# A two-layer hybrid decoder in float32: transition from attention to MLP, and the tail, in another order

## Chip, cores and metric

One core of a Trainium2 chip. The metric is the device time of one execution in microseconds, the median of three runs. A profile was taken of one further execution; all times in the rows come from that one, counted from the start of its span.

## What is computed

Two layers on 256 tokens of width 1024, all in float32. Each layer is an attention part with three kinds of heads, whose outputs form a mixture of 1024 columns (`mix`), and a gated MLP with a causal convolution over tokens. Cut to what matters here:

```python
for i in range(DEPTH):                               # DEPTH = 2
    h = rmsnorm(x, norm1_g[i])
    mix = hybrid_mixer(h, w_in[i], ...)
    x = x + mix @ w_out[i]                           # output projection, 1024 x 1024
    h = rmsnorm(x, norm2_g[i])
    x = x + conv_glu_ffn(h, w_up[i], ..., w_down[i]) # up 1024 -> 2 x 2816, down 2816 -> 1024
return rmsnorm(x, final_g)
```

## The kernel before

The tokens stand as two tiles of 128 rows (t = 0, 1); the residual `xr` stays on the chip. A float32 product is made of three products of rounded parts: each operand is split into a high and a low part, and hi x hi, hi x lo and lo x hi are added up in a PSUM bank (`mm3`, L201, L202, L203). Weights come in pieces through `weight` (L143 to L149): SyncE issues a load into one of 5 staging tiles `st`, ScalarE rounds it to the high part (L147), VectorE subtracts to get the low part (L149), both into one of 8 tiles `hl`. Activations are turned by `transposed`: TensorE transposes 128 x 128 blocks into a bank (L182), ScalarE scales and rounds them (L188), VectorE makes the low part (L189), both into `ahl`.

The source is written stage by stage. A scheduler sets the final order on each engine; engines run their queues in order and wait on each other by semaphores. `dense` holds generators of products that `fill` draws on between other steps, and the scheduler interleaves them with the attention's work.

The places that matter:

- **Output projection**, `out_part`. It is called twice, for the first three weight groups and for the last two (`GROUPS[3:]`). For each half n of the output columns (512) two banks `bd` are open, one per token tile; the groups of weights are walked one by one, with both tiles inside each, and then both banks are added to `xr` (L800).
- **Attention's last product**, 24 matmuls (L848); its output is split by ScalarE (L359) and VectorE (L360), and the second call of `out_part` needs it.
- **`half2(n)`**: squares of the half n of `xr` on ScalarE (L172, by `sumsq`), transposes, evacuations. From the squares GpSimd makes `rstd2` (L165 to L167), and a product with the identity spreads it over columns (L873, `R`).
- **`up(f)`**, one of 11 iterations per layer over the MLP's 2816 hidden columns, 256 at a time: four banks `bu` (two halves s by gate and value, au), each the sum of 8 products of 512 columns (L904) and 8 of 256 (L906). The 8 blocks are the 1024 features, and `ks` says which of them a step takes. In iteration 0 the two banks of s = 0 are walked in two halves of the features, the two of s = 1 whole. Then come convolution, gate and `h_hi`, `h_lo`. `down(f - 1)` follows `up(f)` and adds into four banks `bn`.
- **The tail**, behind the last layer: the last two iterations' down products bank by bank, add (L953), square on ScalarE, multiplication with the final gain (L991), power on GpSimd (L995), scale by ScalarE (L996) and VectorE (L998), and output by two queues (L997, L999), 512 columns each.

```python
order = [(au, s, range(8)) for au in range(2) for s in range(2)]
if f == 0:
    order = [(0, 0, range(4)), (1, 0, range(4)), (0, 0, range(4, 8)), (1, 0, range(4, 8)),
             (0, 1, range(8)), (1, 1, range(8))]
```

Of the kernel before, what the change touches and what calls it, by code (L numbers as in the profile page):

```python
# [76 lines left out]
def trunk(ctx, tc, x, w_in, cmp_w1, cmp_w2, w_out, w_up, w_down, final_g, gains, params, eye, consts_f, consts_b, out):  # L77
# [127 lines left out]
    for i in range(DEPTH):  # L205

        with ExitStack() as es:
# [578 lines left out]
            def out_part(*groups):  # L786
                ks = sum(groups, ())
                for n in range(2):
                    bs = [bank("d"), bank("d")]
                    for g in groups:  # L790
                        wh, wl = weight(piece(w_out[i], (8 * n + g[0]) * 128 * 512, 128, len(g) * 512), len(g), 512)
                        for k in g:
                            for t in range(2):
                                q = slice(t * 128, (t + 1) * 128)
                                mm3(bs[t], mhi[k // 4][:, k % 4, q], mlo[k // 4][:, k % 4, q], wh[:, k - g[0]],
                                    wl[:, k - g[0]], k == ks[0], k == ks[-1])
                        yield
                    for t in range(2):
                        xs = xr[:, t, n * 512:(n + 1) * 512]
                        V.tensor_tensor(xs, bs[t], xs, op=OP.add)  # L800
                yield
# [78 lines left out]
        with ExitStack() as es:  # L880
# [7 lines left out]
            def up(f):  # L888
                wh = [weight(w_up[i, f, au, h], 4, 256)
                      for au in range(2) for h in range(2)]  # L890
                wd = [weight(w_down[i, (2 * f + s) * 128:(2 * f + s + 1) * 128, :], 1, 1024) for s in range(2)]
                order = [(au, s, range(8)) for au in range(2) for s in range(2)]
                if f == 0:
                    order = [(0, 0, range(4)), (1, 0, range(4)), (0, 0, range(4, 8)), (1, 0, range(4, 8)),
                             (0, 1, range(8)), (1, 1, range(8))]
                bs, sums = {}, [mp.tile([128, 2, L], F32, name=n, tag=n) for n in ("sa", "su")]
                for au, s, ks in order:
# [4 lines left out]
                    w = [[z[:, k % 4, s * 128:(s + 1) * 128] for z in wh[2 * au + k // 4]] for k in ks]  # L902
# [38 lines left out]
            def down(fs, which):  # L941
                for n, t in which:
                    for f in fs:
                        h_hi, h_lo, wd = hs[f]
                        for s in range(2):
                            wh, wl = wd[s]
                            q, c = slice(t * 128, (t + 1) * 128), slice(n * 512, (n + 1) * 512)
                            mm3(dn[n, t], h_hi[:, s, q], h_lo[:, s, q], wh[:, 0, c], wl[:, 0, c],
# [88 lines left out]
```

## Time and profile before

| what | value |
|---|---|
| median of 3 runs | 651.7 us (651.59 to 652.59) |
| profiled execution | 651.93 us |
| its span | 650.1 us |
[...]
| TensorE busy | 631.1 us, 97% |
| VectorE busy | 531.6 us, 82% |
| ScalarE busy | 399.3 us, 61% |
| GpSimd busy | 48.0 us, 7% |
| chain that ended last | TensorE 78%, VectorE 14%, ScalarE 3% |

The span runs from the first to the last recorded instruction; 1.8 us of the execution lie around it. Layer 0's transition from attention to MLP lies at about 118 to 154 us, layer 1's at about 435 to 471 us, the tail from 634 us on. A busy share is the time in which at least one instruction's record is open. [...]

### The profile page before, as it was taken

Reading aid. Unit: us, or ns where it says so; the run is one execution under the profiler, and the core shown is the slowest. Engines: PE = TensorE matmul, PEld = TensorE weight load, DVE = VectorE, ACT = ScalarE, POOL = GpSimd, SP = SyncE. Lnnn points to the kernel's source line nnn. Section 1 sums busy time; section 2 is a strip of 40 time slices with the busy share of each in tenths; the row PEclk is TensorE's granted clock in tenths of the full one; section 3 lists DMA queues with packets and bytes.
Section 4 is the critical chain, followed back from the end, with each engine's and each line's share of the span. In section 5 each row is a group of like instructions: output and inputs, shape, how many; then the busy total and the mean of one; then the engine's idle time right before and its main releaser. Section 6 shows DMA issues by size and latency. Waiting matters only on the chain.

```text
span 650.1 us, 10491 instructions
## 1 busy us (share of the span) xinstructions
PE 631.1 (97%) x3694; PEld 538.3 (83%) x3694; DVE 531.6 (82%) x1180; ACT 399.3 (61%) x773; POOL 48.0 (7%) x115
## 2 busy tenths in 40 slices
PE   7989999999999999999999999999999999999995
PEld 6978887778888888888898888867788888888884
DVE  5989999786877778888787799987598787777773
ACT  6666578666555555555575666785665555555533
POOL 0322210000000000000020241000000000000002
PEclk9999999999999999999999999999999999999998
DMA  8971424454666666655466425235367666566601
GB/s 282 331 237 50 148 65 115 161 172 143 203 196 195 192 191 185 189 189 166 121 182 219 144 70 167 83 106 169 115 180 233 190 183 191 191 194 195 193 2 65
DMA packets 32500, 107.28 MB, mean 165 GB/s; under 512 B 3776, under 2 KB 4032, under 8 KB 31936
## 3 DMA queue, kind: packets, MB, share of 16 engines
q1 hardware_dynamic: 31536, 104.77, 51.5%
q0 software_dynamic: 336, 1.05, 0.4%
q10 hardware_dynamic: 576, 0.79, 0.4%
q8 instruction: 29, 0.48, 0.3%
q14 instruction: 23, 0.19, 0.1%
HBM read 105.55 MB, written 1.05 MB: 164 GB/s over the span
## 4 chain that ended last, share of the span: by engine, by line
PE 78%; DVE 14%; ACT 3%; issue 2%; POOL 1%; DMA 1%; POOLq 0%; SPq 0%; DVEq 0%; ACTq 0%
PE bu L904 24%; PE bu L906 13%; PE bn L201 6%; PE bn L202 6%; PE bn L203 6%; PE bd L201 5%; PE bd L203 4%; PE bd L202 4%; DVE hl L149 4%; PE bt L365 1%; PE bs L345 1%; DVE acc L477 1%; DVE P L753 1%; ACT hl L147 1%; DVE m L476 1%
## 5 line engine op out<-in xcount | busy, mean ns | idle before, releaser
L149 DVE TENSOR_TENSOR hl<-st,hl 128x1024 fp32r<-128x1024 f32 (+3 forms) x208 | 232.1, 1120 | 58.6 <-ACT hl L147 58.1
L147 ACT CAST hl<-st 128x1024 fp32r<-128x1024 f32 (+3 forms) x208 | 201.4, 972 | 120.1 <-PE bn L203 43.5
L904 PE MATMUL bu<-ahl,hl 128*128 128x512 f32 x704 | 177.9, 393 | 2.0 <-DVE ahl L189 2.0
L904 PEld LDWEIGHTS bu<-ahl,hl 128*128 128x128 f32 x704 | 127.2, 189 | 25.9 <-DVE ahl L189 2.8
L906 PEld LDWEIGHTS bu<-ahl,hl 128*128 128x128 f32 x704 | 96.7, 190 | 7.1
L906 PE MATMUL bu<-ahl,hl 128*128 128x256 f32 x704 | 99.3, 282 | 0.0
L201 PE MATMUL bd<-hl,ahl 128*128 128x384 f32 (+2 forms) x256 | 92.6, 366 | 1.9 <-ACT hl L147 1.0
L202 PE MATMUL bd<-hl,ahl 128*128 128x384 f32 (+2 forms) x256 | 91.6, 358 | 0.4 <-DVE hl L149 0.4
L203 PE MATMUL bd<-hl,ahl 128*128 128x384 f32 (+2 forms) x256 | 91.5, 357 | 0.0
L201 PE MATMUL bn<-hl,h_hi 128*128 128x512 f32 x176 | 69.0, 392 | 0.1
L202 PE MATMUL bn<-hl,h_hi 128*128 128x512 f32 x176 | 68.7, 391 | 0.0
L203 PE MATMUL bn<-hl,h_lo 128*128 128x512 f32 x176 | 68.5, 389 | 0.0
L909 ACT COPY cross<-bu 128x256 f32<-128x256 f32 x88 | 32.5, 370 | 39.9 <-PE bu L906 39.6
L201 PEld LDWEIGHTS bd<-hl,ahl 128*128 128x128 f32 x256 | 48.1, 189 | 9.9 <-ACT hl L147 2.6
L202 PEld LDWEIGHTS bd<-hl,ahl 128*128 128x128 f32 x256 | 48.3, 189 | 3.8 <-issue 1.1
L203 PEld LDWEIGHTS bd<-hl,ahl 128*128 128x128 f32 x256 | 48.2, 188 | 3.4 <-issue 1.2
L921 DVE SCALAR_TENSOR_TENSOR c<-a,cols,c 128x255 f32<-128x255 f32 (+1 forms) x88 | 40.0, 481 | 7.5 <-ACT c L919 6.3
L203 PEld LDWEIGHTS bn<-hl,h_lo 128*128 128x128 f32 x176 | 33.0, 188 | 7.3 <-DVE h_lo L934 0.3
L201 PEld LDWEIGHTS bn<-hl,h_hi 128*128 128x128 f32 x176 | 33.1, 188 | 7.1 <-ACT h_hi L933 0.9
L202 PEld LDWEIGHTS bn<-hl,h_hi 128*128 128x128 f32 x176 | 33.1, 188 | 6.0
L919 ACT ACTIVATE c<-a,cols 128x256 f32<-128x256 f32 x44 | 24.1, 595 | 13.5 <-DVE a L913 13.5
L910 DVE TENSOR_TENSOR sa<-bu,cross 128x256 f32<-128x256 f32 x44 | 18.4, 417 | 6.5 <-ACT cross L909 4.4
(235 smaller groups left out, 781.8 us busy)
## 6 DMA issues: line engine op xcount, KB each, us to landing
st<-in_w_up_dram SPq DMA_DIRECT2D x88, 512.0 KB, 4.0
st<-in_w_down_dram SPq DMA_DIRECT2D x44, 512.0 KB, 4.3
st<-in_w_in_dram SPq DMA_DIRECT2D x40, 384.0 KB, 4.0
st<-in_w_out_dram SPq DMA_DIRECT2D x12, 512.0 KB, 3.8
w<-in_cmp_w_dram SPq DMA_DIRECT2D x4, 1024.0 KB, 8.4
st<-in_w_in_dram SPq DMA_DIRECT2D x8, 360.0 KB, 3.4
st<-in_w_in_dram SPq DMA_DIRECT2D x8, 336.0 KB, 3.4
st<-in_w_out_dram SPq DMA_DIRECT2D x8, 256.0 KB, 3.1
```

Source lines behind the costliest of these rows:

```text
L147: S.copy(hv, sv)
L149: V.tensor_sub(lv, sv, hv.bitcast(F32))
L201: PE.matmul(b, ahi, whi, start=first, stop=False)
L202: PE.matmul(b, ahi, wlo, start=False, stop=False)
L203: return PE.matmul(b, alo, whi, start=False, stop=last)
L345: PE.matmul(b[:, o:o + nk], qa, ka, start=True, stop=True)
L904: PE.matmul(o, wa, hhl[k // 4][:, k % 4].rearrange("p z t -> p (z t)"), start=k == 0, stop=False)
L906: PE.matmul(o[:, :L], wl, hhi[k // 4][:, k % 4, :], start=False, stop=k == 7)
L909: S.copy(cross, o[:, L:])
L910: V.tensor_tensor(sums[au][:, s], o[:, :L], cross, op=OP.add)
L919: S.activation(c[:, o:o + 256], a[:, o:o + 256], AF.Identity, bias=cw[3], scale=cw[2])
L921: V.scalar_tensor_tensor(c[:, o + d:o + 256], a[:, o:o + 256 - d], cw[w], c[:, o + d:o + 256], op0=OP.mult, op1=OP.add)
```

## The change

- `out_part`: the last two groups of a half n are walked token tile by token tile. Both groups' products of t = 0 are made, its bank is added, and then the same for t = 1. (For the second call, which has two groups, that is all of it.) One `fill` step less is drawn before `half2`.
- `half2`: the transposes are written ahead of the squares, and the last evacuations are returned as `ready`.
- `up(0)`: the weights come as (gate, first half of the features), (value, first half), (gate, second half), (value, second half), and the latter two are cast only behind `ready`. All four banks take the first half of the features, then all four the second.
- Tail: the bank (1, 1) is closed two iterations early and added (L965 there); its last two iterations go into fresh banks `bu`, in two halves of 256 columns. The last square is made on VectorE. The scaled output is split as 384 columns (ScalarE, SyncE's queue) and 640 (VectorE, ScalarE's queue).

```diff
             def out_part(*groups):
...
                     for g in groups:
+                        ws[g] = weight(piece(w_out[i], (8 * n + g[0]) * 128 * 512, 128, len(g) * 512), len(g), 512)
+                        if g in groups[:-2]:
                             for t in range(2):
+                                products(t, g)
+                            yield
                     for t in range(2):
+                        for g in groups[-2:]:
+                            products(t, g)
                         xs = xr[:, t, n * 512:(n + 1) * 512]
                         V.tensor_tensor(xs, bs[t], xs, op=OP.add)
+                        yield
...
-            fill(3)
+            fill(2)
...
             def half2(n):
+                for k0 in (0, 2):
+                    last = transposed(bank, xr, gain2[i], hhi, hlo, 4 * n + k0, 2)
                 for t in range(2):
                     sumsq(ssq, t, n)
-                for k0 in (0, 2):
-                    transposed(bank, xr, gain2[i], hhi, hlo, 4 * n + k0, 2)
+                return [z.ins for z in last]
...
-            half2(0)
+            ready = half2(0)
...
             def up(f):
-                wh = [weight(w_up[i, f, au, h], 4, 256)
-                      for au in range(2) for h in range(2)]
+                wh = {}
+                for au, h in ((0, 0), (1, 0), (0, 1), (1, 1)) if f == 0 else ((0, 0), (0, 1), (1, 0), (1, 1)):
+                    wh[au, h] = weight(w_up[i, f, au, h], 4, 256, behind=ready if (f, h) == (0, 1) else (None, None))
...
                 if f == 0:
-                    order = [(0, 0, range(4)), (1, 0, range(4)), (0, 0, range(4, 8)), (1, 0, range(4, 8)),
-                             (0, 1, range(8)), (1, 1, range(8))]
+                    order = [(au, s, ks) for ks in (range(4), range(4, 8)) for s in range(2) for au in range(2)]
...
+                    f1 = NF - 3 if i == DEPTH - 1 and (n, t) == (1, 1) and into is None else NF - 1
...
+            add(1, 1)
...
+                pieces = [(0, 0, 512), (1, 0, 512)] if t == 0 else [(0, 0, 512), (1, 0, 256), (1, 256, 512)]
+                for j, (n, a, b) in enumerate(pieces):
+                    last = j == len(pieces) - 1
+                    o = None if b - a == 512 else bank("u1")[:, :b - a]
+                    down(fs, [(n, t)], slice(a, b), o)
+                    xs = add(n, t, slice(a, b), o)
...
+                    if last and t:
+                        V.scalar_tensor_tensor(junk[:, :b - a], xs, 1.0, xs, op0=OP.mult, op1=OP.mult,
+                                               accum_out=sq[:, j:j + 1])
+                    else:
+                        S.activation(junk[:, :b - a], xs, AF.Square, accum_out=sq[:, j:j + 1])
...
+                S.activation(y[:, 0:384], y[:, 0:384], AF.Copy, scale=r)
+                nc.sync.dma_start(out[0, t * 128:(t + 1) * 128, 0:384], y[:, 0:384])
+                V.tensor_scalar(y[:, 384:D], y[:, 384:D], r, None, op0=OP.mult)
+                nc.scalar.dma_start(out[0, t * 128:(t + 1) * 128, 384:D], y[:, 384:D])
```

How the order moves. TensorE, layer 0, from the last product of the output projection to the second bank of `up(0)` (`bd` is the projection's bank, `bu` one of `up`, `bt` a transpose's; lines 904 and 906 are 914 and 916 after the change, 182 is the transposes). Before:

```order
L203 MATMUL bd<-hl,ahl 128x512
L904 MATMUL bu_1862<-ahl,hl 128x512
L904 MATMUL bu_1871<-ahl,hl 128x512
L904 MATMUL bu_1902<-ahl,hl 128x512
L904 MATMUL bu_1924<-ahl,hl 128x512
L182 MATMUL bt<-ident,xr 128x128
L904 MATMUL bu_1862<-ahl,hl 128x512 x2
L182 MATMUL bt<-ident,xr 128x128
L904 MATMUL bu_1862<-ahl,hl 128x512
L906 MATMUL bu_1862<-ahl,hl 128x256 x2
L182 MATMUL bt<-ident,xr 128x128 x6
L906 MATMUL bu_1862<-ahl,hl 128x256 x2
```

With the change:

```order
L203 MATMUL bd<-hl,ahl 128x512
L182 MATMUL bt<-ident,xr 128x128 x2
L914 MATMUL bu_1862<-ahl,hl 128x512 x4
L916 MATMUL bu_1862<-ahl,hl 128x256 x3
L182 MATMUL bt<-ident,xr 128x128 x6
L916 MATMUL bu_1862<-ahl,hl 128x256
L914 MATMUL bu_1871<-ahl,hl 128x512 x4
L916 MATMUL bu_1871<-ahl,hl 128x256 x4
L914 MATMUL bu_1880<-ahl,hl 128x512 x4
L916 MATMUL bu_1880<-ahl,hl 128x256 x4
```

Two transposes of the second half now stand ahead of the first up product, which starts with four products of one bank instead of one of each of the four; the banks follow one another, each with the first four blocks of the features alone.

ScalarE, layer 0, from the split of the attention's last output (L359) to the first banks of `up(0)`: casts of weights (L147), squares (L172), evacuations of transposes (L188), the spread row scale (L875, then L884) and evacuations of `up` (L909, then L919). Before:

```order
L359 CAST ahl<-bo 128x2x256
L147 CAST hl<-st 128x1024 x4
L172 ACTIVATE junk,ssq<-xr 128x512 x2
L147 CAST hl<-st 128x1024
L188 ACTIVATE ahl<-bt,cols 128x256 x2
L147 CAST hl<-st 128x1024
L188 ACTIVATE ahl<-bt,cols 128x256 x2
L172 ACTIVATE junk,ssq<-xr 128x512 x2
L188 ACTIVATE ahl<-bt,cols 128x256 x4
L875 COPY R<-bt 128x256
L909 COPY cross<-bu_1862 128x256
L909 COPY cross<-bu_1871 128x256
```

With the change:

```order
L359 CAST ahl<-bo 128x2x256
L172 ACTIVATE junk,ssq<-xr 128x512 x2
L188 ACTIVATE ahl<-bt,cols 128x256 x4
L147 CAST hl<-st 128x1024
L172 ACTIVATE junk,ssq<-xr 128x512
L147 CAST hl<-st 128x1024 x2
L172 ACTIVATE junk,ssq<-xr 128x512
L188 ACTIVATE ahl<-bt,cols 128x256 x2
L147 CAST hl<-st 128x1024 x2
L188 ACTIVATE ahl<-bt,cols 128x256 x2
L147 CAST hl<-st 128x1024 x2
L884 COPY R<-bt 128x256
```

The four casts ahead of the squares and the cast amid the first evacuations have gone behind them; four of the casts now stand among the squares and evacuations of the second half.

VectorE, the tail's second token tile: adds to the residual (L953, then L965), gain (L991, then L1022), sum of the means (L994, then L1018), square (L1012), scale (L998, then L1026). Before:

```order
L953 TENSOR_TENSOR xr<-bn_5262,xr 128x512
L953 TENSOR_TENSOR xr<-bn_5264,xr 128x512
L991 TENSOR_TENSOR y_6976<-xr,fg 128x512
L994 SCALAR_TENSOR_TENSOR fin_6973<-ssq,fin_6972 128x1
L998 TENSOR_SCALAR y_6976<-y_6976,fin_6974 128x512
```

With the change:

```order
L965 TENSOR_TENSOR xr<-bn_5262,xr 128x512
L965 TENSOR_TENSOR xr<-bu_6997,xr 128x256
L1022 TENSOR_TENSOR y<-xr,fg 128x256
L1018 SCALAR_TENSOR_TENSOR fin_6975<-fins_6977,fin_6974 128x1
L965 TENSOR_TENSOR xr<-bu_7015,xr 128x256
L1012 SCALAR_TENSOR_TENSOR junk,fins_6977<-xr 128x256
L1018 SCALAR_TENSOR_TENSOR fin_6976<-fins_6977,fin_6975 128x1
L1022 TENSOR_TENSOR y<-xr,fg 128x256
L1026 TENSOR_SCALAR y<-y,finr_6978 128x640
```

The second add has become two of 256 columns, from banks of `up`; the last one is followed by its square on VectorE, and its gain stands behind the sum instead of ahead of it.

## Rows read from the trace of the kernel before

**Rows 1.** Busy time by stretch: start:end, length, busy us (count) per engine, PEclk, DMA share, GB/s.
```profile
128.00:154.00 26.00, 24.35 (x129) 19.58 (x128) 17.17 (x26) 16.43 (x30) 2.42 (x11) 1.00 0.45 139
154.00:300.00 146.00, 146.00 (x779) 126.11 (x778) 121.06 (x176) 86.02 (x129) 0.00 (x0) 1.00 0.63 194
```

**Rows 2.** TensorE's timeline, layer 0: start us, us, line, operation, out<-in, count [idle before].
```profile
127.98 0.50 PE L203 MATMUL bd<-hl,ahl 128*128 128x512 f32 x1
...
130.16 0.47 PE L201 MATMUL bd<-hl,ahl 128*128 128x512 f32 x1 [0.29 <-DVE xr L800]
...
134.13 0.39 PE L203 MATMUL bd<-hl,ahl 128*128 128x512 f32 x1
134.63 0.50 PE L201 MATMUL bd<-hl,ahl 128*128 128x512 f32 x1
...
137.96 0.82 PE L182 MATMUL bt<-ident,xr 128*128 128x128 f32 x6
138.53 0.48 PE L202 MATMUL bd<-hl,ahl 128*128 128x512 f32 x1
...
139.53 0.39 PE L203 MATMUL bd<-hl,ahl 128*128 128x512 f32 x1
140.91 1.21 PE L904 MATMUL bu<-ahl,hl 128*128 128x512 f32 x4 [0.99 <-DVE ahl L189]
...
154.03 2.00 PE L904 MATMUL bu<-ahl,hl 128*128 128x512 f32 x8
```

**Rows 3.** Chain of waits, layer 0: start us, us, engine, tile, line.
```profile
128.10 0.60 ACT ahl L359
128.72 0.69 DVE ahl L360
...
138.16 1.06 ACT hl L147
139.24 0.77 DVE hl L149
...
140.38 0.87 DVE ahl L189 x2
...
150.67 0.95 PE bu L906 x8
```

**Rows 4.** TensorE's timeline, layer 1.
```profile
447.48 0.47 PE L201 MATMUL bd<-hl,ahl 128*128 128x512 f32 x1 [0.18 <-DVE xr L800]
...
471.33 2.00 PE L904 MATMUL bu<-ahl,hl 128*128 128x512 f32 x8
```

**Rows 5.** Timeline of the tail, last layer.
```profile
643.07 0.39 PE L203 MATMUL bn<-hl,h_lo 128*128 128x512 f32 x1
643.50 0.69 DVE L953 TENSOR_TENSOR xr<-bn,xr 128x512 f32<-128x512 f32 x1 [1.89 <-PE bn L203]
...
644.29 0.63 ACT L172 ACTIVATE junk<-xr 128x512 bf16<-128x512 f32 x1 [1.86 <-DVE xr L953]
644.82 0.19 ACT L172 ACTIVATION_READ_ACCUMULATOR junk<-xr 128x1 f32 x1
...
645.95 0.72 ACT L996 ACTIVATE y<-y,fin 128x512 f32<-128x512 f32 x1 [0.94 <-POOL fin L995]
...
646.69 0.34 SPq L997 DMA_DIRECT2D out_dram<-y  x1
```

**Rows 6.** ScalarE's timeline, layer 0: evacuations of two transposes.
```profile
139.11 0.83 ACT L188 ACTIVATE ahl<-bt,cols 128x256 fp32r<-128x256 f32 x2
```

**Rows 7.** Timeline of SyncE's DMA queue, layer 0.
```profile
131.77 1.59 SPq L143 DMA_DIRECT2D st<-in_w_up_dram  x2
```

**Rows 8.** DMA issues, 154 to 300 us: tile, queue, count, size, median us to landing.
```profile
st<-in_w_up_dram SPq DMA_DIRECT2D x34, 512.0 KB, 4.2
```

**Rows 9.** Costliest groups of the page: out<-in count | busy us, mean ns | idle before.
```profile
L910 DVE TENSOR_TENSOR sa<-bu,cross 128x256 f32<-128x256 f32 x44 | 18.4, 417 | 6.5 <-ACT cross L909 4.4
```

**Rows 10.** Line 251: duration ns min/median/max, first and last start.
```profile
L251 DVE SCALAR_TENSOR_TENSOR junkv<-xr x2: 678/684/691, 14.5 to 15.2; 128x512 bf16<-128x512 f32 x2
```

More of the change, by code (lines that the diff above doesn't have):

```diff
@@ L900, in up @@
                         o = bs[au, s] = bank(f"u{au}")
-                    w = [[z[:, k % 4, s * 128:(s + 1) * 128] for z in wh[2 * au + k // 4]] for k in ks]
+                    w = [[z[:, k % 4, s * 128:(s + 1) * 128] for z in wh[au, k // 4]] for k in ks]
                     for k, (wa, _) in zip(ks, w):
@@ L939, in trunk, with down @@
                     dn[n, t] = bank(f"n{n}")
-            def down(fs, which):
+            def down(fs, which, part=slice(0, 512), into=None):
                 for n, t in which:
+                    f1 = NF - 3 if i == DEPTH - 1 and (n, t) == (1, 1) and into is None else NF - 1
                     for f in fs:
@@ L994, in trunk @@
-                V.scalar_tensor_tensor(m1, ssq[:, t, 1:2], 1.0 / D, m0, op0=OP.mult, op1=OP.add)
-                G.tensor_tensor(r, m1, neghalf[:, 0:1], op=OP.pow)
-                S.activation(y[0], y[0], AF.Copy, scale=r)
-                nc.sync.dma_start(out[0, t * 128:(t + 1) * 128, 0:512], y[0])
-                V.tensor_scalar(y[1], y[1], r, None, op0=OP.mult)
-                nc.scalar.dma_start(out[0, t * 128:(t + 1) * 128, 512:1024], y[1])
+                m = [keep.tile([128, 1], F32, name=f"fin{j}{t}") for j in range(3)]
@@ new lines, in trunk @@
+                sq = keep.tile([128, 3], F32, name=f"fins{t}")
+                r = keep.tile([128, 1], F32, name=f"finr{t}")
+                y = mp.tile([128, D], F32, name="y", tag="y", bufs=2)
+                pieces = [(0, 0, 512), (1, 0, 512)] if t == 0 else [(0, 0, 512), (1, 0, 256), (1, 256, 512)]
[4 more added lines that the diff above has]
+                    xs = add(n, t, slice(a, b), o)
+                    c = slice(n * 512 + a, n * 512 + b)
+                    junk = keep.tile([128, 512], BF, name="junk", tag="junk", bufs=1)
+                    if last and t:
[3 more added lines that the diff above has]
+                        S.activation(junk[:, :b - a], xs, AF.Square, accum_out=sq[:, j:j + 1])
+                    mj = None
+                    if j:
+                        mj = V.scalar_tensor_tensor(m[j], sq[:, j:j + 1], 1.0 / D, m[j - 1], op0=OP.mult, op1=OP.add)
+                    else:
+                        G.tensor_scalar(m[0], sq[:, 0:1], 1.0 / D, EPS, op0=OP.mult, op1=OP.add)
+                    with after(mj.ins if last else None):
+                        (V if j else G).tensor_mul(y[:, c], xs, fg[:, c])
```

36 lines of the change are left out of this document (13 added, 23 removed).

## The prediction, made before the changed kernel was run

> **What bounds the kernel now.** The engine totals come first: TensorE is busy 97% of the span (the table above), so what can be won is where it stands still. The busy time by stretch says where. In the MLP loop (154 to 300 us) it never idles: 146.00 of 146.00. Between attention and MLP of layer 0 it is busy 24.35 of 26.00, at a granted clock of 1.00 [rows 1]. "Busy" hides more standstill: a matmul's record lasts 0.39 us, while the next one starts 0.23 later. So a product is charged at its pitch: seventeen steps lie between 130.16 and 134.13, the first about 0.1 longer because it follows a break, which leaves 0.228 for 512 columns [rows 2]; for 256 columns it is 0.119, eight in 0.95 [rows 3].
>
> The chain of waits through that stretch names the causes [rows 3]. At 128.10 ScalarE and then VectorE empty the attention's last output (0.60, 0.69), the residual adds of the previous pair of banks stand behind them on VectorE, and TensorE's next product starts at 130.16. At 138.16 a weight piece is rounded on ScalarE (1.06) and subtracted on VectorE, ahead of the last evacuations of the first transposes; TensorE resumes at 140.91. In TensorE's own timeline [rows 2]: seven products from 127.98 (0.33 + 6 x 0.228) let it go on at 129.68, so it waits 0.48; then 0.27 before 134.63 (134.13 + 0.23, another add), and 1.15 before 140.91 (139.53 + 0.23). Layer 1 repeats this: 471.33 stands where 154.03 does, 317.3 later [rows 4]. So there are 1.9 us of plain standstill per layer, and more behind 140.91: from there to 154.03 the products of part 3 would take 12.3 of 13.1. At the end there is a serial tail: last matmul, add, square, power, scale, output [rows 5].
>
> **Part 1, output projection by token tile.** The work is the same, in another order: bank t=0 is closed nine products before t=1. The earlier pair's t=0 add thus runs long before the attention block, and only t=1's is late. One product moves ahead of the attention block, which starts about 0.09 later, and six remain behind it instead of seven: from 128.07, 0.33 + 5 x 0.23 gives 129.56 for the next bank's first product against 130.16. That is **0.60**. (Its third product needs the 0.69 VectorE step, done 129.41 [rows 3], and is due 130.1.) The eighteen products then run to 133.67, where two transposes of tile 0 and three products of the next pair follow (0.2 and 0.79). Six more transposes need tile 1's add: its last product ends 133.83, the add runs from 133.87 to 134.56 (0.69 as in [rows 5]), and they start at 134.66. They take 0.57 (137.96 to 138.53, [rows 2]), and fifteen products later it is 138.73, where the kernel before stood at 139.76. The wait of 0.27 is gone, too, since the add that it was for now runs while tile 1's products do.
>
> **Part 2, transposes and evacuations.** In ScalarE's new order the two squares of half 0 still precede the evacuations, against what the source line suggests; what moves is the weight pieces, which no longer stand ahead of and between the evacuations. A square and its read take 0.72 (644.29 to 645.01, [rows 5]), so tile 1's ends 135.3; four evacuations (0.83 a pair, [rows 6]) with VectorE's four (0.87 a pair, [rows 3]), alternately, end 137.3 and 138.3. TensorE arrives at 138.73, does two transposes (0.13 to 0.19), and starts the up product at **138.86 instead of 140.91**, without a wait.
>
> **Part 3, first MLP iteration in halves over four banks.** Four banks times sixteen matmuls are still 4 x 2.79 = 11.17 (8 x 0.23 + 0.95). With six transposes (0.57), four products of 128 columns for the row scale (0.4, priced like transposes) and some 0.25 of restarts: 138.86 + 12.39 = **151.25 for the second iteration's first product, against 154.03**: gain **2.78**. It holds if half 1 of the features is ready when half 0 of four banks has run, at 145.65. Half 1's ScalarE queue from 137.3: piece 0.95 (138.16 to 139.11, [rows 3, 6]), square 0.72, two pieces, square (tile 1's add ends 140.1) to 141.75, two evacuations 142.6, two pieces 144.5, two evacuations 145.4. VectorE's last correction, needed by the fourth product at 146.33, is done 145.85: half a microsecond to spare. The second square's sum reaches GpSimd at 141.8, well before the row scale.
>
> Weights: two casts now wait for the transposes, so staging buffers come free later and SyncE's next up piece is issued at about 139.55 rather than 131.77 [rows 7]. At 4.2 us to landing [rows 8] and 2.4 for cast and subtraction it is usable at 146.2, due 152.2. The down product of iteration 0 is due 162.4; its activation, pulled forward by earlier sums, is ready about 162.0. This is hidden.
>
> **Layer 1.** Three products move ahead of the attention block; by the same walk its first bank starts 446.72 instead of 447.48, 0.76 earlier, then the same steps: 446.72 + (151.25 - 129.56) = 468.41 against 471.33, gain **2.9**. Both gains stay, since in the loops behind TensorE has no idle time to catch up with [rows 1].
>
> **Part 4, the tail.** 24 half products for 12 whole: 24 x 0.119 = 2.86 against 12 x 0.228 = 2.74, so the last product ends 0.13 later, 643.60. Then add at 256 columns 0.42 (the nearest row of that shape, 417 ns) instead of 0.69; square on VectorE, bounded by 0.34 (half of 684 ns) and 0.68, taken as 0.42 with its 0.08 read, instead of ScalarE 0.63 + 0.19 and two crossings; power unchanged; scale of 384 columns between 0.54 (three quarters of 0.72) and 0.72, say 0.61 [rows 5, 9, 10]. Output is issued at 646.1 to 646.2 instead of 646.69, and what follows (3.4 us) I leave unchanged: gain **0.5**, between 0.2 and 0.8. The early add (0.68) falls into VectorE's idle time in the loop (121.06 of 146.00 busy, [rows 1]); without that cover it would cost 0.6.
>
> [...]
>
> **Sum.** 2.78 + 2.9 + 0.5 = 6.2 from the profiled execution's 651.93: **645.7**. That execution is 0.2 above the median of 651.7; from the median it would be 645.5. I say 645.7, as hand walks miss restarts.
>
> **Rivals.**
> - *Half 1 is late.* Two weight pieces stand between its evacuations on ScalarE, three on VectorE ahead of the last. The margin is 0.5; one piece more in the way (1.14 on VectorE, 139.24 to 140.38) costs 0.65 per layer, two 1.8: **647.0 to 649.3**. For: both queues are in order, and exactly such a piece made the 1.15 wait [rows 3]. Against: the order has them counted. Chance 0.18.
> - *The gain is caught up.* The loops behind could be bound by weights or VectorE, and the layer's lead absorbed, leaving the tail: **651.2**, no change. Against: TensorE busy all of 146.00 us, while VectorE rests 25. Chance 0.05. That the change doesn't do what it says is partly so (squares before evacuations), but in the sum.
> - *Slower: late weights.* The next three up pieces are issued from 139.55 on, nearly 8 us later, for a loop that starts 2.8 earlier. If they came p us apart, the third would be usable at 139.55 + 3p + 2.4, due at 157.76 (two groups of 2.79 and four products behind 151.25). At p = 4.2, in single file, there are 3.2 us to spare [rows 8]; a stall begins at 5.3, and from **p = 6.2** it exceeds the 2.8 won. At p = 7 each layer loses 2.4 over before: **656**. Chance 0.05.
>
> **How the numbers follow.** Forecast as walked, 644.8 to 646.7 with the bounds of the tail and 0.4 of restarts per layer: 0.72. Half 1 late: 0.18. These two and a lucky tail make the range 644.5 to 649.0, which leaves out the two small rivals and the end of the first. A measurement of this kernel can tell about 0.2%, 1.3 us, from no change. Faster by more: 0.72 + 0.18 = 0.90; within: 0.05; slower: 0.05.
>
> **What would show it.** Right: no wait in TensorE's timeline before the first bank behind the attention block, the first up product within 0.3 us of the last transposes, and 21.7 us from that bank's first product to the second iteration; loops fully busy; output issued about 2.5 us after the last matmul instead of 3.2. Wrong: a wait on VectorE's corrections between the two halves of the first iteration (first rival), idle time on TensorE in the loop behind (second), or casts waiting for landings there (third).

## The result, and the profile after

The changed kernel took **647.15 us** (median of 4 runs, 646.7 to 648.37) against 651.67 of the kernel before (four runs, too): ratio 0.9923, 95% interval 0.9904 to 0.9942. That is 0.8% faster, inside the range of 644.5 to 649.0, 1.45 us above the predicted 645.7, and 0.45 above the upper end of what the prediction gives as walked (646.7). A repeat gave 646.67, against 652.26 of the kernel before on the same chip, ratio 0.9911 [0.9897, 0.9924]. The profiled execution took 647.47 with a span of 645.7 (TensorE busy 97%, VectorE 83%, ScalarE 61%).

The part ahead of the change is the same code in both kernels, but in this execution it ends about 1 us later. Busy time around the waits on the first weight loads, first of the changed kernel, then of the one before (stretch, length, busy us of TensorE, its weight loads, VectorE, ScalarE, GpSimd; clock, DMA share, GB/s):

```profile
22.00:28.60 6.60, 5.68 (x40) 5.08 (x39) 4.80 (x12) 3.90 (x9) 0.29 (x1) 1.00 0.99 372
```

```profile
22.00:28.60 6.60, 6.60 (x48) 6.39 (x47) 5.90 (x14) 5.05 (x12) 0.02 (x1) 1.00 0.98 374
```

TensorE stands still for 0.92 us at a DMA share of 0.99, while ScalarE waits for the load of a weight piece:

```profile
23.85 0.79 ACT L147 CAST hl<-st 128x720 fp32r<-128x720 f32 x1 [1.15 <-DMA st<-in_w_in_dram]
```

So absolute times of two traces can't be compared. At about 110 us, ahead of anything that was changed, the same products start 0.95 later in this trace (110.17 against 109.22); this is the start's lag below. All executions below are cut at five marks: the start of the last 336-column product of layer 0's input projection (the loads' mark, 27.58 before), the second MLP iteration's first product in layer 0 [rows 2] and in layer 1 [rows 4], the last matmul's end, and the end of the span.

TensorE's timeline of the changed kernel, the places that answer to [rows 2] and [rows 4]:

```profile
130.53 0.39 PE L201 MATMUL bd<-hl,ahl 128*128 128x512 f32 x1
...
135.56 0.87 PE L182 MATMUL bt<-ident,xr 128*128 128x128 f32 x6
136.19 0.49 PE L201 MATMUL bd<-hl,ahl 128*128 128x512 f32 x1
...
139.50 0.39 PE L203 MATMUL bd<-hl,ahl 128*128 128x512 f32 x1
139.74 0.38 PE L182 MATMUL bt<-ident,xr 128*128 128x128 f32 x2
139.87 1.18 PE L914 MATMUL bu<-ahl,hl 128*128 128x512 f32 x4
...
146.64 1.09 PE L914 MATMUL bu<-ahl,hl 128*128 128x512 f32 x4
...
152.26 1.55 PE L914 MATMUL bu<-ahl,hl 128*128 128x512 f32 x6
...
445.07 0.39 PE L201 MATMUL bd<-hl,ahl 128*128 128x512 f32 x1
...
466.80 2.00 PE L914 MATMUL bu<-ahl,hl 128*128 128x512 f32 x8
```

No row has a wait. The first product of the bank behind the attention block starts 130.53 (129.58 without the start's lag of 0.95; 129.56 was predicted), the up products 139.87 (138.92; 138.86), the second iteration 152.26 (151.31; 151.25). The busy time by stretch of the changed kernel agrees [rows 1]:

```profile
128.00:151.50 23.50, 23.50 (x137) 19.74 (x132) 17.90 (x26) 15.66 (x31) 3.83 (x11) 1.00 0.45 145
151.50:300.00 148.50, 148.50 (x791) 128.23 (x791) 122.58 (x180) 86.55 (x130) 0.00 (x0) 1.00 0.62 193
```

The tail of the changed kernel, with what answers to [rows 5]:

```profile
637.65 1.31 POOL L1022 TENSOR_TENSOR y<-xr,fg 128x512 f32<-128x512 f32 x1 [1.27 <-DVE xr L965]
638.14 1.09 DVE L1022 TENSOR_TENSOR y<-xr,fg 128x256 f32<-128x256 f32 x1
638.80 0.28 PE L203 MATMUL bu<-hl,h_lo 128*128 128x256 f32 x1
639.04 0.25 POOL L1020 TENSOR_SCALAR fin<-fins 128x1 f32<-128x1 f32 x1
639.32 0.16 DVE L1018 SCALAR_TENSOR_TENSOR fin<-fins,fin 128x1 f32<-128x1 f32 x1
639.40 0.42 DVE L965 TENSOR_TENSOR xr<-bu,xr 128x256 f32<-128x256 f32 x1
...
640.39 0.42 DVE L1022 TENSOR_TENSOR y<-xr,fg 128x256 f32<-128x256 f32 x1
640.56 0.66 POOL L1023 TENSOR_TENSOR finr<-fin,neghalf 128x1 f32<-128x1 f32 x1 [1.27 <-DVE fin L1018]
641.25 0.61 ACT L1024 ACTIVATE y<-y,finr 128x384 f32<-128x384 f32 x1 [2.33 <-POOL finr L1023]
...
641.84 0.37 ACTq L1027 DMA_DIRECT2D out_dram<-y  x1
641.90 0.34 SPq L1025 DMA_DIRECT2D out_dram<-y  x1
```

The last matmul ends 639.08. The last add starts 0.32 later, where it took 0.04 before (643.46 to 643.50). Ahead of it VectorE holds a sum (639.32) that waited for GpSimd's queue and that multiplication of 1.31. The power on GpSimd (L1023) takes 0.66, with the moved gain product of VectorE beside it. In the kernel before, where that product stood ahead of the sum, it took 0.56:

```profile
645.36 0.56 POOL L995 TENSOR_TENSOR fin<-fin,neghalf 128x1 f32<-128x1 f32 x1 [2.10 <-DVE fin L994]
```

From the last matmul's end to the end of the span it is 6.62, against 6.64 before: nothing was won there.

The stretches between the five marks (us, one profiled execution of each kernel; medians of the runs):

| kernel | loads' mark | to iteration 2, layer 0 | to the same, layer 1 | to last matmul's end | to the end | median |
|---|---|---|---|---|---|---|
| before | 27.58 | 126.45 | 317.30 | 172.13 | 6.64 | 651.67 |
| changed | 28.58 | 123.68 | 314.54 | 172.28 | 6.62 | 647.15 |
| changed, again | 28.27 | 123.67 | 314.55 | 172.28 | 6.63 | 646.67 |
| tail alone | 27.65 | 126.40 | 317.38 | 172.31 | 6.66 | 652.16 |
| parts 1 to 3 | 27.97 | 123.68 | 314.57 | 172.17 | 6.71 | 646.99 |
| part 1 alone | 29.30 | 123.71 | 314.50 | 172.13 | 6.66 | 646.99 |
| part 2 alone | 27.31 | 125.25 | 316.53 | 172.16 | 6.65 | 650.11 |
| parts 2 and 3 | 27.38 | 124.80 | 315.98 | 172.79 | 6.65 | 649.43 |
| no "behind" | 27.28 | 123.82 | 314.62 | 172.31 | 6.57 | 646.47 |
| half 1 delayed | 27.43 | 127.29 | 318.46 | 172.43 | 6.59 | 654.33 |
| sums behind | 27.35 | 123.69 | 314.55 | 172.31 | 6.80 | 646.62 |
| even output | 28.83 | 123.73 | 314.61 | 172.29 | 6.34 | 646.82 |
| gain on VectorE | 27.26 | 123.71 | 314.54 | 172.28 | 6.41 | 646.21 |
| part 1, mended tail | 27.27 | 123.71 | 314.53 | 172.29 | 6.30 | 646.06 |

Read down the columns, kernels with the same code in a stretch agree within 0.1, but for the last loop of "parts 2 and 3" (172.79) and of "half 1 delayed" (172.43), while the loads' mark scatters over 2 us. The span is given to 0.1 us, so a difference of less than 0.1 in the last stretch says nothing.

### The profile page after: what moved, and what is told of

It reads as the page before. It is cut to its first block, busy times and chain, and to the rows that moved or that the text cites. A ratio compares the mean times of both kernels' runs of the same rounds, so it can differ in the third digit from the quotient of the medians.

```text
span 645.7 us, 10509 instructions
## 1 busy us (share of the span) xinstructions
PE 629.2 (97%) x3706; PEld 539.3 (84%) x3706; DVE 534.0 (83%) x1186; ACT 396.4 (61%) x773; POOL 51.6 (8%) x115
## 4 chain that ended last, share of the span: by engine, by line
PE 77%; DVE 14%; ACT 3%; DMA 2%; issue 2%; POOL 1%; POOLq 0%; ACTq 0%; DVEq 0%
PE bu L914 24%; PE bu L916 13%; PE bn L201 6%; PE bn L202 6%; PE bn L203 6%; PE bd L201 4%; PE bd L203 4%; PE bd L202 4%; DVE hl L149 4%; DMA st<-in_w_in_dram 2%; PE bt L365 1%; PE bs L345 1%; DVE acc L477 1%; DVE P L753 1%; DVE m L476 1%
## 5 line engine op out<-in xcount | busy, mean ns | idle before, releaser
L147 ACT CAST hl<-st 128x1024 fp32r<-128x1024 f32 (+3 forms) x208 | 200.8, 971 | 111.4 <-PE bn L203 43.7
L201 PE MATMUL bn<-hl,h_hi 128*128 128x512 f32 x172 | 67.5, 392 | 0.1
L202 PE MATMUL bn<-hl,h_hi 128*128 128x512 f32 x172 | 67.2, 391 | 0.0
L203 PE MATMUL bn<-hl,h_lo 128*128 128x512 f32 x172 | 66.9, 389 | 0.0
L919 ACT COPY cross<-bu 128x256 f32<-128x256 f32 x88 | 32.5, 369 | 40.4 <-PE bu L916 40.1
L201 PEld LDWEIGHTS bn<-hl,h_hi 128*128 128x128 f32 x172 | 32.4, 188 | 6.9 <-ACT h_hi L943 0.9
L202 PEld LDWEIGHTS bn<-hl,h_hi 128*128 128x128 f32 x172 | 32.4, 188 | 5.9
```

The source lines that it names most:

```text
L147: S.copy(hv, sv)
L201: PE.matmul(b, ahi, whi, start=first, stop=False)
L202: PE.matmul(b, ahi, wlo, start=False, stop=False)
L203: return PE.matmul(b, alo, whi, start=False, stop=last)
L919: S.copy(cross, o[:, L:])
```

## The experiments

Each kernel was timed in five rounds beside the kernel before on the same chip. The row of each in the table above belongs to its reading.

### The change again, and its parts

**The changed kernel again**, unchanged.

> The changed kernel once more, unaltered. In its first trace it ran 0.95 us behind the kernel before already at 112 us, in code that both share, after a wait for a load of the input weights at about 25 us. Theory (scatter of the first loads, nothing of the change): the median comes to 646.5 to 647.2 again, single runs spread by 1 to 2 us, and in this trace the wait at 25 us is longer or shorter than before by some tenths at random. Rival (the change delays the start): the product at 25.45 us of the kernel before stands at 26.3 again, and no run comes below 646.5.

646.67 (646.19 to 647.21), ratio 0.9911 [0.9897, 0.9924]. Its stretches repeat those of the first execution within 0.01. Two of its five runs lie below 646.5 (646.19 and 646.34), as expected if the late start is scatter and not an effect of the change.

**The tail alone:** `down`, `add` and the last block from the changed kernel, all else before.

```diff
+            add(1, 1)
...
+                pieces = [(0, 0, 512), (1, 0, 512)] if t == 0 else [(0, 0, 512), (1, 0, 256), (1, 256, 512)]
...
```

> The kernel before with the new tail alone. Prediction's term: gain 0.5, 651.2. Theory after the first trace: the issue of the output moves 0.25 us earlier, but the landing takes 2.8 instead of 2.5, so the span from the last matmul's start to the end is the same within 0.2 and the time is 651.4 to 651.8; on GpSimd the multiplication by the gain and on VectorE the one of 256 columns again overlap and take 1.3 and 1.1, and the last add starts 0.3 behind the last matmul instead of 0.04.

652.16 (651.81 to 653.02), ratio 1.0 [0.9992, 1.0009]. Products end 0.18 later (172.31 against 172.13), as 24 half products stand for 12 whole, and the rest of the tail is as long as before. The tail is worth nothing; I had expected 651.4 to 651.8.

**Parts 1 to 3 without the tail:** the changed kernel with `down`, `add` and the last block from before.

```diff
-            add(1, 1)
...
-                pieces = [(0, 0, 512), (1, 0, 512)] if t == 0 else [(0, 0, 512), (1, 0, 256), (1, 256, 512)]
...
```

> The changed kernel with the old tail. Theory: both transitions gain 2.7 each, all of the change: 646.2 to 646.8, equal to the changed kernel within 0.4. Rival (tail carries 0.5): 0.5 slower than the changed kernel.

646.99, ratio 0.9915 [0.9902, 0.9928]: the whole gain, 2.77 and 2.73 in the two layers.

**Parts 2 and 3 alone:** the transposes' order and the MLP's halves in the kernel before; projection and tail as before.

```diff
+                    wh[au, h] = weight(w_up[i, f, au, h], 4, 256, behind=ready if (f, h) == (0, 1) else (None, None))
...
+                    order = [(au, s, ks) for ks in (range(4), range(4, 8)) for s in range(2) for au in range(2)]
```

> The kernel before with the new order of transposes, weights and products in the first MLP iteration, but the old output projection. If the parts add up as in the prediction's sum (projection about 1.0 of the 2.78, the rest 1.75): 648.2. If either part alone already removes the wait of 1.15 at 140.91 (they overlap): about 2.0 to 2.2 per layer, 647.3 to 647.7.

649.43 (648.72 to 651.39), ratio 0.996 [0.9947, 0.9972], slower than either expectation: 1.65 and 1.32 in the two layers, and 0.66 of it lost again behind layer 1's mark, of which a wait for a late activation at 480.52 explains 0.33; the rest was not followed.

**Part 1 alone:** the projection by token tile in the kernel before, nothing else.

```diff
+                        if g in groups[:-2]:
...
+                        for g in groups[-2:]:
+                            products(t, g)
...
-            fill(3)
+            fill(2)
```

> The kernel before with the new output projection alone (two last groups token tile by token tile; its last step one fill earlier). If the parts simply add, it holds what the transition without it lacked: the kernel with the MLP part alone took 649.4, the one with both 647.0, so about 2.4 less than before, some 649.8. If each of the two parts alone removes the same wait before the first up product, they overlap: the first up product starts near 139.9 on its own axis (before 140.9), a gain near 1.9 per layer, and about 648.0 in all.

646.99 (646.75 to 648.08), ratio 0.9922 [0.991, 0.9935]. The stretches are 123.71 and 314.50: **part 1 alone brings the whole gain**, 2.74 and 2.80. Both expectations (649.8 and 648.0) were too small a gain. TensorE's timeline of this kernel, whose start is 1.72 later than that of the kernel before:

```profile
136.34 0.88 PE L182 MATMUL bt<-ident,xr 128*128 128x128 f32 x6
136.97 0.48 PE L201 MATMUL bd<-hl,ahl 128*128 128x512 f32 x1
...
140.27 0.39 PE L203 MATMUL bd<-hl,ahl 128*128 128x512 f32 x1
140.50 0.62 PE L912 MATMUL bu<-ahl,hl 128*128 128x512 f32 x2
```

its ScalarE at the same place, the evacuation last:

```profile
134.91 1.05 ACT L147 CAST hl<-st 128x1024 fp32r<-128x1024 f32 x1 [2.09 <-PE bd L203]
...
136.49 1.03 ACT L147 CAST hl<-st 128x1024 fp32r<-128x1024 f32 x1
...
138.05 0.82 ACT L188 ACTIVATE ahl<-bt,cols 128x256 fp32r<-128x256 f32 x2
```

and the first corrections on VectorE:

```profile
138.69 0.87 DVE L189 SCALAR_TENSOR_TENSOR ahl<-bt,cols,ahl 128x256 fp32r<-128x256 f32 x2
```

Two casts still stand among the squares ahead of the evacuations, and TensorE doesn't wait for them: between the last of the first transposes (the next product starts 136.97) and the up product (140.50) it has fifteen projection products, 3.5 us. Before there were five [rows 2]: 138.53 to 139.76, and then the wait. What stands between is hardly shorter: the corrections begin 1.72 behind the transposes here (138.69 - 136.97), and 1.85 before (140.38 - 138.53, [rows 3]). So the step was not sped up, it was covered.

Less the 1.72 the first up product starts 138.78, 2.13 earlier than before (140.91). The other 0.61 of the 2.74 comes behind it: to the second iteration it takes 12.51 (140.50 to 153.01) instead of 13.12.

**Part 2 alone:** the same `half2` order (not shown here) and the weight pieces behind the transposes, with product order, projection and tail of before.

```diff
+                wh = [weight(w_up[i, f, au, h], 4, 256, behind=ready if (f, h) == (0, 1) else (None, None))
+                      for au in range(2) for h in range(2)]
```

> The kernel before with part 2 alone: squares behind the transposes in the code and the weight pieces of the first MLP iteration's second half rounded behind the first transposes; projection, product order and tail as before. Parts 2 and 3 together gained 1.65 and 1.32 in the two layers (649.4). If part 3, the halves over four banks, matters beside part 2, TensorE waits here for half 1 after two banks (needed near 146.5, last correction near 146.8): 0.3 to 1 less gain in each layer, 650.0 to 651.4. If part 2 does it all: 649.2 to 649.7.

650.11 (649.6 to 652.25), ratio 0.997 [0.996, 0.998]: 1.20 and 0.77. Where part 1 is missing, part 2 is thus worth, in layer 0, about what the prediction saw in it, the wait of 1.15; its two edits, the squares and the casts, were not tried apart. The halves (part 3) add 0.45 and 0.55 beside part 2; beside part 1 they add nothing (part 1 alone against parts 1 to 3: 0.03 one way, 0.07 the other). TensorE of this kernel still waits for a correction of the first transposes, and not, as I had expected if the halves matter, for half 1:

```profile
140.32 0.30 PE L182 MATMUL bt<-ident,xr 128*128 128x128 f32 x1 [0.33 <-DVE ahl L189]
```

### The casts' place, and the margin of half 1

**Without "behind"** in the changed kernel: casts may stand ahead of and between the evacuations again.

```diff
-                    wh[au, h] = weight(..., behind=ready if (f, h) == (0, 1) else (None, None))
+                    wh[au, h] = weight(..., behind=(None, None))
```

> The changed kernel without the order by which the two weight pieces of the first MLP iteration's second half are rounded behind the first transposes: the scheduler then puts three casts ahead of the squares, one between them and a square between the evacuations. By the prediction's reading (a weight piece ahead of an evacuation makes TensorE wait 1.15) up products start about 1 later in each layer, 1.5 to 2.3 in all: 648.5 to 649.3. Rival (the squares and the projection by token tile already clear the way, the casts find staging early enough): the first up product within 0.3 of the changed kernel's, 646.5 to 647.5.

646.47 (646.38 to 647.05), ratio 0.9914 [0.9901, 0.9928]; stretches 0.14 and 0.08 longer than with it. The prediction's reading, that the casts in front of the evacuations make the wait, falls for the kernel that has part 1: its ScalarE has a cast right ahead of the first evacuation, and TensorE's timeline shows no wait.

```profile
134.56 1.03 ACT L147 CAST hl<-st 128x1024 fp32r<-128x1024 f32 x1
135.50 0.83 ACT L188 ACTIVATE ahl<-bt,cols 128x256 fp32r<-128x256 f32 x2
```

**Half 1 delayed**, to see how near the first rival was: two more evacuations into a scratch tile ahead of each of half 1.

```diff
+            extra = None
+            for _ in range(more):
...
+                extra = S.activation(junk[:, :256], bj, AF.Copy, scale=g).ins
+            with after(extra):
+                l0 = S.activation(h[:, j, :], bj, AF.Copy, scale=g)
```

> The changed kernel with each ScalarE evacuation of the second half of the features (the first MLP iteration's half 1) preceded by two more of the same into a scratch tile: eight more ScalarE instructions of 0.36 in each layer, and four casts drift ahead of them in the scheduler's order. In the changed kernel's trace the last correction of half 1 ends 146.06 and would be waited for only from about 147.3; here it should end near 150.3. First rival of the prediction (TensorE takes half 1 bank by bank, so any delay beyond the margin is a wait): 3 lost in each layer, 653 in all, and 3.7 by the margin of 0.5 as predicted. My reading now (four open banks let TensorE take the features that are ready in all four banks first, so only the last of them is waited for): 1 to 1.5 in each layer, 649 to 650.

654.33 (653.74 to 654.93), ratio 1.0031 [1.002, 1.0042]: 0.3% slower than the kernel before. TensorE of this kernel now waits three times for half 1 and once for the row scale, whose squares were pushed back as well:

```profile
146.41 1.20 PE L919 MATMUL bu<-ahl,hl 128*128 128x512 f32 x4 [0.16 <-DVE ahl L194]
148.41 1.20 PE L919 MATMUL bu<-ahl,hl 128*128 128x512 f32 x4 [0.80 <-DVE ahl L194]
150.31 0.50 PE L919 MATMUL bu<-ahl,hl 128*128 128x512 f32 x1 [0.70 <-DVE ahl L194]
...
152.53 0.71 PE L887 MATMUL bt<-ident,rstd 128*128 128x128 f32 x4 [0.77 <-POOL rstd L167]
```

The last corrections of half 1, first of the changed kernel, then of this one:

```profile
145.18 0.88 DVE L189 SCALAR_TENSOR_TENSOR ahl<-bt,cols,ahl 128x256 fp32r<-128x256 f32 x2
```

```profile
149.77 0.48 DVE L194 SCALAR_TENSOR_TENSOR ahl<-bt,cols,ahl 128x256 fp32r<-128x256 f32 x1
```

The last one is done 11.43 behind the first up product (138.82 to 150.25), in the changed kernel 6.19 (139.87 to 146.06): 5.24 later. The changed kernel needs it 7.47 behind (its fourth product from 146.64 on), so 1.28 is its margin, and 5.24 less 1.28 would be 3.96 lost; the two layers lost 3.61 and 3.92. My expectation of 1 to 1.5, by four open banks that take what is ready, was wrong: the scheduler did take the products across the banks, but the corrections came 2 us apart and four products take 0.93, so the wait was only cut in pieces, and the row scale's came on top. The first rival's mechanism is real, and its price is of the right size, though the row scale's wait is in the loss as well. In the changed kernel it did not occur.

### The tail

**Sums behind:** the last token tile's first two gains to GpSimd, their sums to VectorE and, in the source, behind the last add.

```diff
-                        mj = V.scalar_tensor_tensor(m[j], sq[:, j:j + 1], 1.0 / D, m[j - 1], op0=OP.mult, op1=OP.add)
+                        for k in ((), (1,), (1, 2))[j] if t else (1,):
+                            if last:
+                                mj = V.scalar_tensor_tensor(m[k], sq[:, k:k + 1], 1.0 / D, m[k - 1], op0=OP.mult, op1=OP.add)
...
-                        G.tensor_scalar(m[0], sq[:, 0:1], 1.0 / D, EPS, op0=OP.mult, op1=OP.add)
+                        (V if t else G).tensor_scalar(m[0], sq[:, 0:1], 1.0 / D, EPS, op0=OP.mult, op1=OP.add)
...
-                        (V if j else G).tensor_mul(y[:, c], xs, fg[:, c])
+                        (V if (last if t else j) else G).tensor_mul(y[:, c], xs, fg[:, c])
```

> The changed kernel; in the tail of the last token tile the first two pieces' gain products go to GpSimd and their two sums to VectorE, so VectorE's last add waits for no multiplication of GpSimd. My theory (the last add came 0.28 late because a sum on VectorE waited behind GpSimd's 1.31 us multiplication, and the 256-wide product on VectorE took 1.09 instead of about 0.42 while GpSimd multiplied): add 0.04 to 0.1 after the last matmul instead of 0.32, output issued 2.5 to 2.6 after it instead of 2.82, 0.25 less in all, which the span shows only after the start's own scatter of 0.6 is taken off. Rival (the add is late for TensorE's own end): add as late as it was, no difference.

A miss: 646.62 (ratio 0.9915 [0.9902, 0.9929]), and the tail got longer, 6.80. The last matmul ends 637.90, the add comes 0.48 later. The scheduler still put the sum ahead of it, and one element per partition took 0.69 beside GpSimd's two multiplications (0.16 elsewhere):

```profile
636.46 1.99 POOL L1024 TENSOR_TENSOR y<-xr,fg 128x512 f32<-128x512 f32 x2 [1.27 <-DVE xr L965]
...
637.77 0.69 DVE L1020 SCALAR_TENSOR_TENSOR fin<-fins,fin 128x1 f32<-128x1 f32 x1 [0.39 <-ACT junk L1015]
638.38 0.41 DVE L965 TENSOR_TENSOR xr<-bu,xr 128x256 f32<-128x256 f32 x1
```

**Even output:** 512 and 512 columns in the changed kernel's last transfers, not 384 and 640.

```diff
-                nc.sync.dma_start(out[0, t * 128:(t + 1) * 128, 0:384], y[:, 0:384])
+                nc.sync.dma_start(out[0, t * 128:(t + 1) * 128, 0:512], y[:, 0:512])
...
```

> The changed kernel with the two output transfers of the last stage even again, 512 and 512 columns as before, instead of 384 and 640. If the landing grows with the larger transfer (2.7 to 2.8 with 384/640, 2.1 and 2.5 with 512/512): ScalarE's scale 0.1 longer, landing 0.2 to 0.4 shorter, so last matmul to end 6.3 to 6.5 instead of 6.62. Rival (the landing scatters whatever the size): 6.6 to 6.8.

646.82 (ratio 0.9916 [0.9903, 0.993]) with a loads' mark of 28.83; the tail is 6.34, 0.28 shorter, as expected. Of that, 0.15 lies ahead of the first issue (2.61 behind the last matmul instead of 2.76), and 0.13 behind it. The output's issues, first of the changed kernel, then of this one (queue, count, size, us to landing):

```profile
out_dram<-y ACTq DMA_DIRECT2D x1, 320.0 KB, 2.7
out_dram<-y SPq DMA_DIRECT2D x1, 192.0 KB, 2.8
```

```profile
out_dram<-y ACTq DMA_DIRECT2D x1, 256.0 KB, 2.1
out_dram<-y SPq DMA_DIRECT2D x1, 256.0 KB, 2.5
```

Although SPq's transfer is smaller in the change, it lands later. From the first issue of the pair (641.84) to SPq's landing (641.90 + 2.8) it is 2.86; before, it was 2.72 (646.47, and 646.69 + 2.5). The landings are read to a tenth.

**Gain on VectorE:** even output, and the 512-column gain of the last token tile on VectorE, so that GpSimd multiplies nothing there.

```diff
-                        (V if j else G).tensor_mul(y[:, c], xs, fg[:, c])
+                        (V if j or t else G).tensor_mul(y[:, c], xs, fg[:, c])
...
```

> The changed kernel with even output (512 and 512 columns) and the tail's last gain product of 512 columns on VectorE instead of GpSimd, so that GpSimd multiplies nothing while VectorE works. My theory (VectorE and GpSimd slow each other): VectorE's 256-wide product back to 0.42 from 1.0, the last add at most 0.15 after the last matmul instead of 0.24 to 0.48, output issued 2.6 to 2.7 after it, and last matmul to end 6.1 to 6.2 against 6.62 of the changed kernel and 6.34 with even output alone. Rival (the 1.0 is what this shape takes, or VectorE has no room for 0.69 more): add 0.3 or later, 6.4 or more.

646.21 (645.95 to 646.93), ratio 0.9909 [0.9894, 0.9924]; tail 6.41. The tail was expected at 6.1 to 6.2. One half of the theory holds: the 256-column product takes 0.43 again. The other does not: the last matmul ends 637.79 and the add still comes 0.26 later, now behind a sum that waits for ScalarE's square.

```profile
637.30 0.43 DVE L1022 TENSOR_TENSOR y<-xr,fg 128x256 f32<-128x256 f32 x1
637.36 0.42 ACT L1015 ACTIVATE junk<-xr 128x256 bf16<-128x256 f32 x1 [0.34 <-DVE xr L965]
...
637.98 0.16 DVE L1018 SCALAR_TENSOR_TENSOR fin<-fins,fin 128x1 f32<-128x1 f32 x1 [0.24 <-ACT junk L1015]
638.05 0.42 DVE L965 TENSOR_TENSOR xr<-bu,xr 128x256 f32<-128x256 f32 x1
```

**Part 1 and a mended tail:** the changed kernel without parts 2 and 3, and in its tail even output, the last token tile's gains on VectorE, and that sum ordered behind the last square.

```diff
...
+                        with after(z.ins):
+                            V.scalar_tensor_tensor(m[1], sq[:, 1:2], 1.0 / D, m[0], op0=OP.mult, op1=OP.add)
...
```

> The kernel before with part 1 (projection by token tile) and a tail mended by what the runs showed: even output, all gain products of the last token tile on VectorE, and the sum of its second piece behind the last add and square, so that the last add has nothing in front of it; parts 2 and 3 are left as before. If part 1 alone carries the transition and the last add was late for that sum: last add 0.04 to 0.1 after the last matmul, output issued 2.65 to 2.75 after it on the queue that is last, last matmul to end 6.1 to 6.2 (6.62 in the changed kernel), and 610.3 to 610.5 from the first load-bound product to the last matmul, as in the changed kernel: 645.7 to 646.5, 0.4 to 0.5 under the changed kernel on equal starts. If the last add waits for something else: as late as it was, 646.6 to 647.2.

646.06 (645.89 to 647.1), ratio 0.9917 [0.9903, 0.9931]. The add follows the last matmul's end (637.80) by 0.04, but the moved sum takes its own place in the chain (638.72 to 638.91 below), and the tail is 6.30, not 6.1 to 6.2:

```profile
637.84 0.43 DVE L963 TENSOR_TENSOR xr<-bu,xr 128x256 f32<-128x256 f32 x1
638.37 0.43 DVE L1010 SCALAR_TENSOR_TENSOR junk<-xr 128x256 bf16<-128x256 f32 x1
...
638.72 0.15 DVE L1013 SCALAR_TENSOR_TENSOR fin<-fins,fin 128x1 f32<-128x1 f32 x1
638.91 0.16 DVE L1018 SCALAR_TENSOR_TENSOR fin<-fins,fin 128x1 f32<-128x1 f32 x1
```

From loads' mark to the end it takes 616.83 against the changed kernel's 617.12, without parts 2 and 3. In the medians 0.3 us can't be told from the scatter of the start.

## Why the prediction was right, and where it was off

**The sum.** Predicted 2.78 + 2.9 + 0.5 = 6.2. Measured by the stretches: 2.77 in layer 0, 2.76 in layer 1, and -0.13 for the tail (0.15 more products, 0.02 less behind them), 5.4 in all. The profiled execution came out at 647.47, 1.77 over the forecast: 1.00 from the start's loads, 0.14 from layer 1, 0.63 from the tail. The time as walked, with its own bounds, ended at 646.7, and the median of 647.15 lies above that (the repeat's 646.67 just below). It is inside the range because the range was stretched to 649.0 for a late half 1, which did not occur; that much is luck.

- **Layer 0** was right to 0.1 at each of its three marks. What fixes the time is TensorE's work without a gap: every kernel with part 1, but for the one with half 1 delayed (127.29), needs 123.67 to 123.82 up to the second iteration, in different orders on ScalarE and VectorE.
- **Layer 1:** I took 0.14 too much. Its first bank behind the attention block starts at 445.07, while the walk, less the lead of 1.85 that this trace had ahead of that change (426.94 against 428.80 for the same product), gives 444.87.
- **The attribution failed.** In the walk, part 1 brings 1.03 of layer 0's 2.78 (138.73 instead of 139.76), part 2 another 1.02 (the wait of 1.15, less the two transposes moved ahead), and part 3 the last 0.73. Part 2's reason was "what moves is the weight pieces, which no longer stand ahead of and between the evacuations". Measured, part 1 alone gives 2.74, part 2 alone 1.20, parts 2 and 3 alone 1.65, and letting the casts stand ahead again costs 0.14. The walk held the right fact, "fifteen products later", and did not price it: fifteen products behind the transposes cover 3.5 us of casts, evacuations and corrections, five cover 1.2. So the parts are two ways to take away the same wait and don't add. What limited both is the floor of TensorE's own work. The total of layer 0 came out because the walk followed the order that all the parts have together, in which that wait is counted once.
- **The tail failed** in three steps. "Output is issued at 646.1 to 646.2", about 2.5 behind the last matmul, counted each operation on VectorE and left out that the sum ahead of the last add depends on GpSimd's queue: the add came 0.28 later than the same step before, and the second of the two issues, SyncE's, which that figure is for, 2.82 behind the last matmul. "Power unchanged" left out that the gain product now stands beside it: 0.66 instead of 0.56. And "what follows (3.4 us) I leave unchanged": the first issue is 2.76 behind the last matmul (641.84 - 639.08) instead of 3.01, 0.25 earlier, but the uneven pair needs 2.86 from its first issue to the last landing instead of 2.72, and from the first issue to the end of the span it is 3.86 (645.7 - 641.84) instead of 3.63 (650.1 - 646.47): 0.23 of the 0.25 is given back.
- **Halving the last piece** was priced right. The add took 0.42 (predicted 0.42), more than half of the 0.69 that it takes at 512 columns, the square 0.42 with 0.08 read (the same), the scale 0.61 (0.61), and the 24 half products 0.15 to 0.18 more (0.13).
- **Rivals.** Half 1 late didn't occur: the last correction came 6.19 behind the first up product, where 6.99 was walked, which makes the margin 1.28 instead of 0.5; what it would have cost is what the delayed half showed. The gain was not caught up: from layer 1's mark on, changed and unchanged kernel need the same within 0.2, and the 2.77 of layer 0 still stand in front of layer 1. Late weights did not show: one cast waited 0.35 for its landing at 146.80, TensorE for none.

## What to carry to other kernels

When a serial step (transpose, evacuate, correct) stands between two blocks of products, count the independent products that are left behind its trigger. Moving the trigger earlier in TensorE's order hid here both the casts and the order of the halves, and left the other two parts worth nothing measurable beside it. Price parts that remove the same wait once, against the floor of the engine that waited. In a tail, list for each instruction on the last engine's queue what the one in front of it waits for, other engines' queues included, and measure an output pair from its first issue to its last landing.

## What the runs showed of the hardware

- **VectorE beside GpSimd.** A 256-column product of `xr` and `fg` took 1.09 us in the changed kernel (from 638.14) and 1.01 with even output (from 638.52), each while GpSimd multiplied 512 columns, and 0.43 where GpSimd multiplied nothing (gain on VectorE, from 637.30); a one-element sum took 0.69 (sums behind, from 637.77) instead of 0.16. Each slow one ended just behind GpSimd's multiplication: 639.23 against 638.96 and 639.53 against 639.26 (0.27 both), 638.46 against 638.45. Not every instruction was longer there: the changed kernel's add of 256 columns from a bank took 0.42 (from 637.68), beside the same multiplication (637.65 to 638.96). It shows the other way, too: GpSimd's power of one element took 0.56 to 0.58 with VectorE idle (the kernel before), 0.66 behind VectorE's 256-column gain product, and 0.99 behind the 512-column one of the first token tile (635.25 to 635.94, the power from 635.39); it ended 0.41 and 0.44 behind that product. So in both directions the longer instruction ended 0.01 to 0.44 behind the one that had started first; why it took longer is not shown. A one-element operation in that place is hit, too: the sum lost 0.53. No run here puts the last gain product ahead of the sum again, so whether that would take the 0.10 off the power is not shown.
- **A split pair of outputs is timed from its first issue.** From there to the last landing (read to a tenth) it was 2.72 to 2.73 with 256 and 256 KB, and 2.85 to 2.86 with 320 and 192 KB. From the first issue to the end of the span, all fourteen executions divide by that split: 3.63 to 3.77 in the eight with even halves, 3.81 to 3.90 in the six with uneven ones. Issuing the second transfer earlier (0.06 instead of 0.23 behind the first) bought nothing.
- **The first loads** are where executions of one program differ: 27.26 to 29.30 at the loads' mark over fourteen profiled executions with the same code up to there. Four of them have a wait like the one shown at 23.85 (marks 27.97, 28.27, 28.58, 29.30), in one more the time is lost earlier (28.83), and the other nine lie between 27.26 and 27.65. One and the same chip gave 27.28, 27.35, 28.83 and 29.30. Part 1 alone shows what it does to a time: its profiled execution, with 29.30, is the slowest of its five (648.08; the others 646.75 to 647.27). Whether the mark also hangs on the program, not only on the execution, stays open, since each program but one was profiled once.
